# Adding the causal mask of a prompt's scores with weights of 64 rows instead of 128

## The chip, the cores and the metric

The kernel runs on one core of a Trainium2 chip. The metric is the device time of one launch in microseconds; before the change the median of three runs is 2850.2 us (2848.51 to 2850.68). The profile shows one execution, whose span from the first to the last instruction is 2845.2 us, at a mean granted TensorE clock of 0.998.

## The reference, cut to what matters

One inference step of a decoder with two layers: a short gated convolution with a feed forward behind it, then differential attention with a feed forward behind it. There are 1024 new prompt tokens and 8 sequences of 8 sample tokens, each with 2048 cached keys and values in pages of 128. The change lies in the attention of the prompt:

```python
s = jnp.einsum('bqhd,bkhd->bhqk', q, k).astype(jnp.float32) * SCALE      # head dim 64, 2 * 8 heads
s = jnp.where(mask[None, None], s, jnp.finfo(jnp.float32).min)           # causal
p = jax.nn.softmax(s, axis=-1)
a = p[:, :, 0] - lam * p[:, :, 1]                                        # the two halves of a head
return jnp.einsum('bhqk,bkhe->bqhe', a, v.astype(jnp.float32))
```

A head has two halves (here c = 0 and c = 1), each with scores and a softmax of its own; their difference weighs the values.

## The kernel before, in words

Nearly all of the time is matmul in float32 with a high and a low part for each operand (three products). The stages follow each other: the convolution and the first feed forward, the projections of the prompt (line L687), the attention of the prompt with the attention of the samples mixed in, the output projection (L140) and the second feed forward.

The attention of the prompt goes over 8 heads and, in each, over 8 blocks of 128 queries (i = 4, 5, 6, 7, 0, 1, 2, 3), so 64 blocks. For a block, `scores` makes for each half a 128 x n matrix in PSUM, n = 128 (i + 1). A half has 64 dimensions, so the contraction has 64 rows: half 0 has its operands in partitions 0 to 63 and half 1 in 64 to 127, and the two matmuls of a pair stand next to each other (L752). Up to n = 512 both halves share one PSUM tile of two banks; above that each half has a tile of two banks, and there are two such tiles in all. The mask is then added by TensorE itself: an identity `idb` of 128 x 128 in bfloat16 as weights, and the mask of the diagonal block `cmask` as the moving operand, accumulated onto the last 128 columns, once for each half (L755). Then VectorE takes the maximum of each row (L757 or L759), ScalarE the exponential (L763), and the result waits. One or two blocks later `mixed` turns it with TensorE (L780) and `values` multiplies with the values (L787); `place` (L806) puts four finished blocks back; `head_turn` (L726) turns the next head's queries and keys.

Between these stand steps of the samples: `step(x)` adds x to a credit, and for each full 1 one step of a generator is recorded, which weighs one page of values (L590, four column tiles of 32) and multiplies one page of keys (L532, eight matmuls in the same tiles). Before the change `step(0.72)` stands behind each of the two masks, so 1.44 steps per block. Pages come through six buffers of 512 KB, and SyncE issues their loads (L511) in a fixed order, each as soon as its buffer is free.

In this stage the order on TensorE, VectorE, ScalarE and GpSimd is set by a scheduler from the order in the program and the dependences; SyncE's queue is kept as written. In the profile a matmul's shape has the part of the array that it uses ahead: `64*128` is 64 rows (a half's scores), `128*128` the whole array, `128*32` a column tile of the samples.

Of the kernel before, what the change touches and what calls it, by code (L numbers as in the profile page):

```python
# [11 lines left out]
BF16 = mybir.dt.bfloat16  # L12
# [6 lines left out]
P = 128  # L19
# [30 lines left out]
def decoder_kernel(ctx: ExitStack, tc: tile.TileContext, i_: dict, o_: dict):  # L50
    nc = tc.nc
    PE, ACT, DVE, POOL, SP = nc.tensor, nc.scalar, nc.vector, nc.gpsimd, nc.sync
# [25 lines left out]
    def load_split(src, width=D, eng=None, sub=None, lo_raw=False):  # L78
        raw = rawp.tile([P, width], F32, name="raw", tag="raw")
        (eng or SP).dma_start(raw, src)  # L80
        hi = wsp.tile([P, width], F32R, name="whi", tag="w")
        lp, tag = (rawp, "raw") if lo_raw else (wsp, "w")
        lo = lp.tile([P, width], F32R, name="wlo", tag=tag)
        split_to(hi, lo, raw, sub)
        return hi, lo, raw

    def passes(ah, al, bh, bl):
        return ((ah, bh), (ah, bl), (al, bh))
# [151 lines left out]

    xsT = cst.tile([P, KT, NS], F32, name="xsT")

    # ------------------------------------------------------------ layer 0
    with tc.tile_pool(name="accp", bufs=1) as accp, \
         ExitStack() as conv_stack, \
         tc.tile_pool(name="pout0", bufs=4, space=PSUM) as pout, \
# [2 lines left out]
        tp = conv_stack.enter_context(tc.tile_pool(name="tp", bufs=1, reuse_waits="tile"))  # L249
        st = stream(accp, "acc")  # L250

        # ---- short convolution
        taps = accp.tile([P, KT, 3], F32, name="taps")
        stT = accp.tile([P, KT, NSEQ, 2], F32, name="stT")
        cpT = accp.tile([P, KT, 2], F32, name="cpT")
# [99 lines left out]
        POOL.dma_start(o_["conv_p"], cpT)  # L355
        POOL.dma_start(o_["conv_s"], csT)

        # ---- feed forward
        def ffn(layer, pin, pout, hp, tp, st, ln):
            def feature(f):  # L360
                sg = tp.tile([P, NT], F32, name="sg", tag="gb", bufs=1)
                hh = hp.tile([P, NT], F32R, name="hh", tag="h")
                hl = hp.tile([P, NT], F32R, name="hl", tag="h")
                hs = hp.tile([P, NS], F32, name="hs", tag="hs", bufs=5)

                def put_g(c0, cw, ps):
                    ACT.activation(sg[:, c0:c0 + cw], ps, AF.Silu)  # L367

                def put_u(c0, cw, ps):
                    cs = slice(c0, c0 + cw)  # L370
                    hf = tp.tile([P, 364], F32, name="hf", tag="hf")
                    DVE.tensor_tensor(hf[:, :cw], ps, sg[:, cs], op=ALU.mult)  # L372
                    split_to(hh[:, cs], hl[:, cs], hf[:, :cw])
                    if c0 == 0:
                        POOL.tensor_copy(hs, hf[:, 0:NS])

                in_type(pin, i_["wfi"][layer, 2 * f], put_g)
                in_type(pin, i_["wfi"][layer, 2 * f + 1], put_u)
                return hh, hl, hs

            run_chunks(pout, st, (2,) * 9 + (4,), feature, i_["wfo"][layer], ln)
# [4 lines left out]
            ffn(0, pin, pout, hp, tp, st,  # L386
                norm(1, tp, accp, "f32", x2_dram, lambda x: SP.dma_start(s2_dram, x)))

    # ------------------------------------------------------------ layer 1 attention
    with tc.tile_pool(name="kvp", bufs=1, reuse_waits="tile") as kvp, \  # L390
         tc.tile_pool(name="ap", bufs=1, reuse_waits="tile") as ap, \
         tc.tile_pool(name="ap2", bufs=2, reuse_waits="tile") as ap2, \
# [8 lines left out]
            return kvp.tile(shape, dtype, name=name, tag=f"kv{next(kv_slot)}")  # L401

        w0 = [load_split(i_["wqkv"][0, kh].rearrange("p k c -> p (k c)"), eng=POOL, lo_raw=kh == 0) for kh in range(2)]
        # constants of this phase
        idb = ap2.tile([P, P], BF16, name="idb", bufs=1)
        cmask = ap2.tile([P, P], BF16, name="cmask", bufs=1)
        smask = ap.tile([P, 120], F32, name="smask")
        sel = ap.tile([P, 4], F32, name="sel")
        cmb = ap.tile([P, NS], F32, name="cmb")
# [10 lines left out]
        ccA = ap.tile([P, 2], F32, name="ccA")  # L420

        def constants():
            for tl, nm in ((idb, "idb"), (cmask, "cmask"), (smask, "smask"), (sel, "sel"), (cmb, "cmb"),
                           (ropp, "ropp"), (rops, "rops"), (ptab, "ptab")):
                SP.dma_start(tl, i_[nm])
            SP.dma_start(gs, i_["subg"])
            SP.dma_start(lamt, i_["lam"].partition_broadcast(P))
            DVE.tensor_scalar(gs, gs, 1.0 - LAM_INIT, None, op0=ALU.mult)
            DVE.tensor_tensor(lpr, lamt[:, 0:4:2, :], lamt[:, 1:4:2, :], op=ALU.mult)
            DVE.tensor_reduce(lsum, lpr, axis=AX.X, op=ALU.add)  # L430
            ACT.activation(lex, lsum, AF.Exp)
            DVE.tensor_tensor(nlam, lex[:, 1:2], lex[:, 0:1], op=ALU.subtract)
            DVE.tensor_scalar(nlam, nlam, LAM_INIT, None, op0=ALU.subtract)
            DVE.scalar_tensor_tensor(ccA, sel[:, 2:4], nlam[:, 0:1], sel[:, 0:2], op0=ALU.mult, op1=ALU.add)
# [9 lines left out]
            DVE.tensor_tensor(vb[..., 8:16], dst[..., 0:8], sin[..., 8:16], op=ALU.mult)  # L444
            DVE.tensor_tensor(x12, va, vb, op=ALU.add)

        # ---- sample tokens: projections folded over two partition halves, then paged attention
        vs = ap.tile([P, 512], F32, name="vs")
        qT = ap.tile([P, 4, P], F32, name="qT")
        kTs = ap.tile([P, 4, P], F32, name="kTs")  # L450
# [208 lines left out]
        def step(x):  # L659
            credit[0] += x  # L660
            while credit[0] >= 1.0:
                credit[0] -= 1.0
                next(samp, None)

        RATE3 = 0.76
        # ---- prompt projections
        with tc.manual_schedule(engines={mybir.EngineType.PE}):
            for pr in range(4):
                for ty, dst in enumerate((q_dram, o_["k_p"], o_["v_p"])):
# [6 lines left out]
                    for tg in range(2):  # L676
# [3 lines left out]
                        for kh, t in [(kh, t) for kh in range(2) for t in range(4)] if first else [(None, t) for t in range(4)]:  # L680
# [3 lines left out]
                            for k in range(KT) if kh is None else range(4 * kh, 4 * kh + 4):  # L684
                                cs = slice((k % 4) * 256, (k % 4) * 256 + 256)
                                for n, (a, b_) in enumerate(passes(xTh, xTl, his[k // 4], los[k // 4])):
                                    PE.matmul(ps[t][:, t % 2, :256], a[:, k, t0:t0 + P], b_[:, cs],  # L687
                                              start=(k == 0 and n == 0), stop=(k == KT - 1 and n == 2),
                                              skip_group_check=True)
# [14 lines left out]
                        cols = slice(pr * 256, pr * 256 + 256)  # L704
                        POOL.dma_start(dst[rows, cols].rearrange("(t p) c -> p t c", p=P), nat)

        # ---- prompt attention
        def head_load(h):
            cols = slice(h * P, h * P + P)
            out = []  # L710
            for src, nm in ((q_dram, "qn"), (o_["k_p"], "kn"), (o_["v_p"], "vn")):
                t = (rawp if nm != "vn" else ap2).tile([P, KT, P], F32, name=nm, tag="raw" if nm != "vn" else "vn")
                POOL.dma_start(t, src[:, cols].rearrange("(t p) c -> p t c", p=P))
                out.append(t)
            return out
# [16 lines left out]
        def scores(q, k, i):  # L732
            n = (i + 1) * P
            nb = 1 if n <= 512 else 2
            w = n // nb
            kf = [x.rearrange("p t c -> p (t c)") for x in k]
            nms = sml.tile([P, 2], F32, name="pnm", tag="pnm")
            l = sml.tile([P, 2], F32, name="pl", tag="pl")
            Ps = []
            ps = pt = None  # L740
            svs = []
            for c in range(2):
                if nb == 2 or c == 0:
                    ps = ps2.tile([P, 2, 512], F32, name="psS2", tag="s2")
                    pt = ap2.tile([P, NP], F32, name="pexp", tag="pr", bufs=4)
                svs.append(ps[:, :, :w] if nb == 2 else ps[:, c:c + 1, :w])
                Ps.append((svs[c], pt[:, :n] if nb == 2 else pt[:, c * 512:c * 512 + n]))
            for bk in range(nb):
                for m, (a, b_) in enumerate(passes(q[0], q[1], kf[0], kf[1])):
                    for c in range(2):  # L750
                        cp = slice(c * 64, c * 64 + 64)
                        PE.matmul(svs[c][:, bk, :], a[cp, i, :], b_[cp, bk * w:bk * w + w],  # L752
                                  start=(m == 0), stop=(m == 2), skip_group_check=True)
            for c in range(2):
                PE.matmul(svs[c][:, nb - 1, w - P:w], idb, cmask, start=False, stop=True, skip_group_check=True)  # L755
                if nb == 2:
                    DVE.tensor_reduce(nms[:, c:c + 1], svs[c], axis=AX.XY, op=ALU.max, negate=True)  # L757
                elif c == 1:
                    DVE.tensor_reduce(nms, ps[:, :, :w], axis=AX.X, op=ALU.max, negate=True)  # L759
                step(RATE4)  # L760
            for c in range(2):
                sv, pv = Ps[c]
                ACT.activation(pv.rearrange("p (b w) -> p b w", b=nb), sv, AF.Exp,  # L763
                               bias=nms[:, c:c + 1], accum_out=l[:, c:c + 1])
            ls, Ps = l, [p_ for _, p_ in Ps]
            rl = sml.tile([P, 2], F32, name="prl", tag="prl")
            DVE.reciprocal(rl, ls)
            r1 = rl[:, 0:1]
            rr = sml.tile([P, 1], F32, name="prr", tag="prr")
            DVE.scalar_tensor_tensor(rr, ls[:, 0:1], rl[:, 1:2], nlam, op0=ALU.mult, op1=ALU.mult)  # L770
            DVE.scalar_tensor_tensor(Ps[0], Ps[1], rr[:, 0:1], Ps[0], op0=ALU.mult, op1=ALU.add)
            return r1, Ps[0]
# [39 lines left out]
        RATE4 = 0.72  # L812
# [27 lines left out]
                place(*done)  # L840
        step(200)

    # ------------------------------------------------------------ attention output, feed forward
    with tc.tile_pool(name="accq", bufs=1, reuse_waits="tile") as accp, \
         tc.tile_pool(name="hq", bufs=8, reuse_waits="tile") as hp, \
         tc.tile_pool(name="tq", bufs=2, reuse_waits="tile") as tp, \
# [109 lines left out]
```

## Time and profile before

| what | value |
|---|---|
| median of the runs | 2850.2 us |
| span of the profiled execution | 2845.2 us |
| median of the runs less that span | 5.0 us |
| TensorE busy in that span | 2810.5 us, 99% |
| VectorE, ScalarE, GpSimd busy | 1190.4, 704.7, 253.7 us |
| first matmul of the prompt's scores to the last mask | 1574.4 to 1937.3 us |
| mask matmuls (L755) | 128, each 219 to 232 ns from start to end |

The profile gives no time of its own for the whole launch of the profiled execution, only its span; what lies around the span is taken as the 5.0 us by which the median is above it. A matmul's duration there reaches from its first operand to its last result, and the next one starts before it ends; so what a matmul costs is read from one start to the next, in the timeline, and not from its duration.

### The profile page before, as it was taken

To read this page: it belongs to the slowest core of one execution; us is meant where nothing else is said; L and a number is where in the kernel's file an instruction comes from. 1 tells how busy PE (TensorE), PEld (TensorE's weight loads), DVE (VectorE), ACT (ScalarE), POOL (GpSimd) and SP (SyncE) were. 2 spreads that over 40 slices of the span, in tenths; PEclk is the share of its full clock that TensorE was granted. 3 is DMA by queue.
4 is the path that set the end of the run, shared out by engine and by line. 5 is a ranking of instruction groups with operands and counts; after the bars stand their busy time and mean duration, and the time that the engine had idled before them with its cause. 6 is when DMAs were issued, how large, how long until landed. Compare 5 with 4: busy or idle time off the path is not lost.

```text
span 2845.2 us, 45546 instructions
## 1 busy us (share of the span) xinstructions
PE 2810.5 (99%) x19092; PEld 2474.1 (87%) x19092; DVE 1190.4 (42%) x2083; ACT 704.7 (25%) x1366; POOL 253.7 (9%) x517
## 2 busy tenths in 40 slices
PE   9999999999999999999999999999999999999998
PEld 9998989999999999879888666667799999999996
DVE  4435373333333332722222566676733333333325
ACT  3111141111111111312221455562311111111111
POOL 0000020000000000311111223231200000000002
PEclk9999999999999999999999999999999999999999
DMA  6111021111111111486777888761211111111102
GB/s 225 39 39 57 25 83 42 44 43 44 45 43 45 45 44 31 137 284 205 268 273 259 290 275 297 275 211 60 75 52 45 45 45 45 45 45 45 45 30 78
DMA packets 87456, 307.50 MB, mean 108 GB/s; under 512 B 10929, under 2 KB 11586, under 8 KB 87250
## 3 DMA queue, kind: packets, MB, share of 16 engines
q1 hardware_dynamic: 76194, 265.45, 27.7%
q0 software_dynamic: 10624, 38.35, 4.1%
q8 instruction: 150, 2.46, 0.4%
q10 hardware_dynamic: 432, 0.79, 0.1%
q14 instruction: 56, 0.46, 0.0%
HBM read 282.46 MB, written 22.09 MB: 107 GB/s over the span
## 4 chain that ended last, share of the span: by engine, by line
PE 93%; DMA 2%; DVE 1%; POOL 1%; ACT 1%; issue 1%; SPq 0%; POOLq 0%; DVEq 0%; ACTq 0%
PE pin L104 46%; PE pout L140 21%; PE psqkv L687 9%; PE psS L752 3%; PE psO L590 3%; PE pso L787 2%; PE psS L532 2%; PE pouts L125 2%; PE psaT L780 1%; PE psq L474 1%; DMA vpg<-cv 1%; PE psS L755 1%; POOL rs_t L93 1%; PE pstr L726 0%; PE ptr L216 0%
## 5 line engine op out<-in xcount | busy, mean ns | idle before, releaser
L104 PE MATMUL pin<-xTh,whi 128*128 128x362 f32 (+1 forms) x2688 | 876.0, 326 | 6.4 <-ACT xTh L75 6.4
L104 PE MATMUL pin<-xTl,whi 128*128 128x362 f32 (+1 forms) x2688 | 875.6, 326 | 0.3 <-DVE xTl L76 0.3
L104 PE MATMUL pin<-xTh,wlo 128*128 128x362 f32 (+1 forms) x2688 | 875.0, 326 | 0.0
L76 DVE TENSOR_TENSOR wlo<-raw,whi 128x1024 fp32r<-128x1024 f32 (+1 forms) x197 | 239.9, 1218 | 687.9 <-PE pin L104 400.7
L104 PEld LDWEIGHTS pin<-xTh,whi 128*128 128x128 f32 x2688 | 505.6, 188 | 7.4 <-ACT xTh L75 6.4
L104 PEld LDWEIGHTS pin<-xTl,whi 128*128 128x128 f32 x2688 | 505.6, 188 | 1.6 <-DVE xTl L76 0.7
L104 PEld LDWEIGHTS pin<-xTh,wlo 128*128 128x128 f32 x2688 | 505.6, 188 | 0.1
L75 ACT CAST whi<-raw 128x1024 fp32r<-128x1024 f32 (+1 forms) x197 | 203.8, 1045 | 729.7 <-PE pout L140 379.0
L140 PE MATMUL pout<-whi,hh 128*128 128x512 f32 x704 | 279.3, 397 | 0.0
L140 PE MATMUL pout<-whi,hl 128*128 128x512 f32 x704 | 278.6, 396 | 0.0
L140 PE MATMUL pout<-wlo,hh 128*128 128x512 f32 x704 | 278.0, 395 | 0.0
L687 PE MATMUL psqkv<-whi,xTh 128*128 128x256 f32 x768 | 222.5, 290 | 0.0
L687 PE MATMUL psqkv<-wlo,xTh 128*128 128x256 f32 x768 | 214.5, 279 | 0.0
L687 PE MATMUL psqkv<-whi,xTl 128*128 128x256 f32 x768 | 214.4, 279 | 0.0
L140 PEld LDWEIGHTS pout<-whi,hh 128*128 128x128 f32 x704 | 132.6, 188 | 45.7 <-issue 14.6
L140 PEld LDWEIGHTS pout<-whi,hl 128*128 128x128 f32 x704 | 132.7, 189 | 31.2 <-issue 1.6
L367 ACT ACTIVATE sg<-pin 128x364 f32<-128x364 f32 x132 | 62.6, 474 | 388.6 <-PE pin L104 388.6
L140 PEld LDWEIGHTS pout<-wlo,hh 128*128 128x128 f32 x704 | 132.6, 188 | 30.1
L687 PEld LDWEIGHTS psqkv<-whi,xTh 128*128 128x128 f32 x768 | 144.5, 188 | 15.6 <-issue 14.5
L372 DVE TENSOR_TENSOR hf<-pin,sg 128x364 f32<-128x364 f32 x132 | 70.4, 533 | 207.0 <-PE pin L104 207.0
L115 DVE TENSOR_TENSOR acc<-acc,pout 128x512 f32<-128x512 f32 x160 | 109.3, 687 | 93.5 <-PE pout L140 93.5
L687 PEld LDWEIGHTS psqkv<-wlo,xTh 128*128 128x128 f32 x768 | 144.7, 188 | 0.0
(216 smaller groups left out, 3236.7 us busy)
## 6 DMA issues: line engine op xcount, KB each, us to landing
kpg<-ck SPq DMA_DIRECT2D x128, 512.0 KB, 5.6
vpg<-cv SPq DMA_DIRECT2D x128, 512.0 KB, 5.0
raw<-wfi SPq DMA_DIRECT2D x88, 512.0 KB, 4.0
raw<-wfo SPq DMA_DIRECT2D x44, 512.0 KB, 3.7
raw<-wqkv POOLq DMA_DIRECT2D x24, 512.0 KB, 5.6
raws<-wqkv SPq DMA_DIRECT2D x24, 512.0 KB, 6.4
raw<-wci SPq DMA_DIRECT2D x23, 512.0 KB, 3.7
acc<-xn SPq DMA_DIRECT2D x8, 512.0 KB, 9.7
```

Of the source, the lines that this page charges most:

```text
L75: ACT.copy(hi, src)
L76: (eng or DVE).tensor_tensor(lo, src, fv(hi), op=ALU.subtract)
L104: PE.matmul(ps[:, :cw], a[:, k * P:(k + 1) * P], b[:, k, c0:c0 + cw], start=(k == 0 and n == 0), stop=(k == KT - 1 and n == 2),)
L115: DVE.tensor_tensor(a, a, ps, op=ALU.add)
L125: PE.matmul(ps[half * NS:half * NS + NS, :], hs, raw[:, half * 512:half * 512 + 512], start=(j == 0), stop=(j == last), skip_group_check=True)
L140: PE.matmul(ps, a[:, t0:t0 + P], b[:, cs], start=(j == 0 and n == 0), stop=(j == last and n == 2))
L367: ACT.activation(sg[:, c0:c0 + cw], ps, AF.Silu)
L372: DVE.tensor_tensor(hf[:, :cw], ps, sg[:, cs], op=ALU.mult)
L532: PE.matmul(ps[32 * t:32 * t + 32, n, :], qp[:, 2 * t + h2, :], kp[:, 2 * t + h2, :], start=(h2 == 0), stop=(h2 == 1), skip_group_check=True)
L590: PE.matmul(O[32 * t:32 * t + 32, :], PT[:, p, 32 * t:32 * t + 32], vp[:, 2 * t:2 * t + 2, :].rearrange("p h d -> p (h d)"), start=(p == 0 ...
L687: PE.matmul(ps[t][:, t % 2, :256], a[:, k, t0:t0 + P], b_[:, cs], start=(k == 0 and n == 0), stop=(k == KT - 1 and n == 2), skip_group_che ...
L752: PE.matmul(svs[c][:, bk, :], a[cp, i, :], b_[cp, bk * w:bk * w + w], start=(m == 0), stop=(m == 2), skip_group_check=True)
```

## The change

`idb` and `cmask` are held twice, in partitions 0 to 63 and in 64 to 127, with their rows 0 to 63 and 64 to 127 side by side; each needs two loads of 64 partitions instead of one. The mask of a half is added by two matmuls with 64 rows of weights each: the first adds rows 0 to 63 of the mask over all 128 columns, the second rows 64 to 127 over the last 64 columns alone, where these rows have something to mask. Half 0 uses partitions 0 to 63 and half 1 partitions 64 to 127, as in the scores. All four stand together, and the steps of the samples, `step(2 * RATE4)`, come behind them. Comment lines were taken out too.

```diff
-        idb = ap2.tile([P, P], BF16, name="idb", bufs=1)
-        cmask = ap2.tile([P, P], BF16, name="cmask", bufs=1)
+        idb = ap2.tile([P, 2, P], BF16, name="idb", bufs=1)
+        cmask = ap2.tile([P, 2, P], BF16, name="cmask", bufs=1)
...
-            for tl, nm in ((idb, "idb"), (cmask, "cmask"), (smask, "smask"), (sel, "sel"), (cmb, "cmb"),
+            for tl, nm in ((idb, "idb"), (cmask, "cmask")):
+                for c in range(2):
+                    SP.dma_start(tl[c * 64:c * 64 + 64], i_[nm].rearrange("(r p) k -> p r k", r=2))
+            for tl, nm in ((smask, "smask"), (sel, "sel"), (cmb, "cmb"),
                            (ropp, "ropp"), (rops, "rops"), (ptab, "ptab")):
                 SP.dma_start(tl, i_[nm])
...
+            for r in range(2):
+                for c in range(2):
+                    cp = slice(c * 64, c * 64 + 64)
+                    PE.matmul(svs[c][:, nb - 1, w - P + 64 * r:w], idb[cp, r, :], cmask[cp, r, 64 * r:],
+                              start=False, stop=(r == 1), skip_group_check=True)
             for c in range(2):
-                PE.matmul(svs[c][:, nb - 1, w - P:w], idb, cmask, start=False, stop=True, skip_group_check=True)
                 if nb == 2:
                     DVE.tensor_reduce(nms[:, c:c + 1], svs[c], axis=AX.XY, op=ALU.max, negate=True)
                 elif c == 1:
                     DVE.tensor_reduce(nms, ps[:, :, :w], axis=AX.X, op=ALU.max, negate=True)
-                step(RATE4)
+            step(2 * RATE4)
```

Where the order on TensorE changes is seen at three places. The lines of the changed kernel are 4 higher from the samples on (L752 is L756 there, L590 L594, L532 L536) and 9 higher behind the masks (L780 is L789, L787 L796); the new masks are L762.

First, TensorE, the third head's block of i = 2. Before:

```order
L752 MATMUL psS_16828<-qtl,qth 128x384 x2
L752 MATMUL psS_16828<-qth,qtl 128x384 x2
L755 LDWEIGHTS idb
L755 MATMUL psS_16828<-cmask,idb 128x128
L590 MATMUL psO<-vpg,PT 32x256 x4
L532 MATMUL psS<-kpg,qpad_9080 32x128 x8
L755 LDWEIGHTS idb
L755 MATMUL psS_16828<-cmask,idb 128x128
L787 MATMUL pso<-vn,aT 128x128
L726 MATMUL pstr<-ident,kn 128x128 x4
```

and in the changed kernel:

```order
L756 MATMUL psS_16874<-qtl,qth 128x384 x2
L756 MATMUL psS_16874<-qth,qtl 128x384 x2
L762 LDWEIGHTS idb
L762 MATMUL psS_16874<-cmask,idb 128x128
L762 LDWEIGHTS idb
L762 MATMUL psS_16874<-cmask,idb 128x128
L762 LDWEIGHTS idb
L762 MATMUL psS_16874<-cmask,idb 128x64
L762 LDWEIGHTS idb
L762 MATMUL psS_16874<-cmask,idb 128x64
L594 MATMUL psO<-vpg,PT 32x256 x4
L536 MATMUL psS<-kpg,qpad_9080 32x128 x8
```

The step of the samples stood between the two masks and now stands behind all four; `pso` (L796 there) follows it.

Second, TensorE, the next block (i = 3), which has two steps of the samples. Before:

```order
L755 LDWEIGHTS idb
L755 MATMUL psS_16922<-cmask,idb 128x128
L590 MATMUL psO<-vpg,PT 32x256 x4
L532 MATMUL psS<-kpg,qpad_9080 32x128 x8
L755 LDWEIGHTS idb
L755 MATMUL psS_16922<-cmask,idb 128x128
L590 MATMUL psO<-vpg,PT 32x256 x4
L532 MATMUL psS<-kpg,qpad_9080 32x128 x8
L787 MATMUL pso<-vn,aT 128x128 x2
```

and in the changed kernel, from the second half of the masks on:

```order
L762 LDWEIGHTS idb
L762 MATMUL psS_16970<-cmask,idb 128x64
L762 LDWEIGHTS idb
L762 MATMUL psS_16970<-cmask,idb 128x64
L594 MATMUL psO<-vpg,PT 32x256 x4
L536 MATMUL psS<-kpg,qpad_9080 32x128 x8
L594 MATMUL psO<-vpg,PT 32x256 x4
L536 MATMUL psS<-kpg,qpad_9080 32x128 x8
L796 MATMUL pso<-vn,aT 128x128 x2
```

The two steps now follow each other with no mask between them.

Third, SyncE, the constants of the attention, before the samples' first loads:

```order
L426 DMA idb<-idb 64x2x128 x2
L426 DMA cmask<-cmask 64x2x128 x2
L171 DMA x_dram<-acc_101 128x1024
L429 DMA smask<-smask 128x120
L429 DMA sel<-sel 128x4
```

Before, the first two rows were one load each, of 128 x 128, at the same place.

## The prediction

> **What bounds the kernel now.** First the page's totals, its chain of work and its rate of transfers by slices; then one stretch of the view by windows, from the first score to the last mask.
>
> ```profile
> span 2845.2 us, 45546 instructions
> PE 2810.5 (99%) x19092; PEld 2474.1 (87%) x19092; DVE 1190.4 (42%) x2083; ACT 704.7 (25%) x1366; POOL 253.7 (9%) x517
> ...
> GB/s 225 39 39 57 25 83 42 44 43 44 45 43 45 45 44 31 137 284 205 268 273 259 290 275 297 275 211 60 75 52 45 45 45 45 45 45 45 45 30 78
> ...
> PE 93%; DMA 2%; DVE 1%; POOL 1%; ACT 1%; issue 1%; SPq 0%; POOLq 0%; DVEq 0%; ACTq 0%
> ```
>
> ```profile
> 1574.00:1938.00 364.00, 358.94 (x3690) 245.97 (x3690) 247.94 (x497) 209.34 (x582) 103.65 (x229) 1.00 0.77 263
> ```
>
> TensorE is busy for 99% of the span and is 93% of the chain that ended last. In the stage of the change, 364 us long, its columns are TensorE 358.94 busy, its weight loads 245.97, VectorE 247.94, ScalarE 209.34, GpSimd 103.65, then the clock (1.00), the share of the DMA engines (0.77) and GB/s (263). No other engine is near full. What TensorE waited for there, by the view of waits:
>
> ```profile
> PE psO L590 <- DMA vpg<-cv: 2.0, 3, 1.3
> PE psS L532 <- DMA kpg<-ck: 1.3, 2, 0.8
> PE pstr L726 <- DVE ost L790: 0.5, 2, 0.2
> PE psaT L780 <- ACT aT L781: 0.4, 1, 0.4
> PE psS L752 <- ACT pexp L763: 0.3, 1, 0.3
> PE psS L752 <- ACT qth L728: 0.2, 1, 0.2
> ```
>
> That is all: 4.7 us of 364. So this stage's length is the sum of the steps from one matmul's start to the next, and what the change takes out of these steps it takes out of the time. But "busy" says little about the steps. The view of waits for the weight loads shows where they are long:
>
> ```profile
> PEld L755 <- issue: 19.5, 75, 0.4
> ```
>
> 75 of the 128 mask matmuls' weight loads start after 0.26 us on average in which they wait for no other engine. The timeline shows what this is (start, duration, instruction, count; the duration is a latency, only starts are compared):
>
> ```profile
> 1700.90 0.28 PE L752 MATMUL psS<-qtl,qth 64*128 64x256 f32 x2
> 1701.02 0.29 PE L752 MATMUL psS<-qth,qtl 64*128 64x256 f32 x2
> 1701.24 0.29 PE L755 MATMUL psS<-cmask,idb 128*128 128x128 bf16 x2
> 1701.45 0.64 PE L590 MATMUL psO<-vpg,PT 128*32 128x256 f32 x8
> ...
> 1706.25 0.33 PE L780 MATMUL psaT<-ident,pexp 128*128 128x128 f32 x1
> 1706.51 0.44 PE L752 MATMUL psS<-qth 64*128 64x384 f32 x2
> 1706.79 0.33 PE L752 MATMUL psS<-qtl,qth 64*128 64x384 f32 x2
> 1706.96 0.34 PE L752 MATMUL psS<-qth,qtl 64*128 64x384 f32 x2
> 1707.23 0.23 PE L755 MATMUL psS<-cmask,idb 128*128 128x128 bf16 x1
> 1707.39 0.64 PE L590 MATMUL psO<-vpg,PT 128*32 128x256 f32 x8
> 1707.84 0.62 PE L532 MATMUL psS<-kpg,qpad 128*32 128x128 f32 x16
> 1708.39 0.23 PE L755 MATMUL psS<-cmask,idb 128*128 128x128 bf16 x1
> 1708.46 0.44 PE L787 MATMUL pso<-vn,aT 128*128 128x128 f32 x2
> ```
>
> A pair of scores of 384 columns takes 0.17 when the next pair has the same shape of array (1706.79 to 1706.96), and 0.27 when a mask over all 128 rows follows (to 1707.23). With 256 columns it is 0.12 against 0.22 (1700.90, 1701.02, 1701.24). The mask in front of a column tile takes 0.16 (1707.23 to 1707.39); in front of a matmul over the whole array 0.07 (1708.39 to 1708.46), though the type changes there too. So **a switch between `64*128`, `128*128` and `128*32` costs about 0.10 us**, and the first score pair behind a switch (1706.51, after a turn over the whole array) takes 0.28 instead of 0.17, another 0.11.
>
> **The change part by part.**
>
> *Switches.* I count, in the two orders on TensorE from the first score to the last mask, the neighbours of different shape: 486 before, 367 after. Of the 486, 94 lead into a mask (64 of them straight from the scores), 73 out of one and 319 stand elsewhere; of the 367 it is 2, 63 and 302. The masks now have the scores' shape, so the switch from scores to mask is gone in all but two places, and a step between two masks no longer makes two switches of its own. 119 switches by 0.10 us are -11.9 us. Only mask, scores and column tiles are read above; that the others cost as much is an assumption for the 17 that vanish elsewhere. Behind a switch, 11 fewer score pairs start (11 by 0.11, -1.2), 10 more `pso` do and 24 fewer groups of pages; none of these last two is priced by a row above, and I put the whole at -1, with -2 and +1 as ends.
>
> *The masks themselves.* Before: two masks and the switch behind them take 0.21 (1701.24 to 1701.45), so one takes about 0.06: 128 by 0.06 is 7.7 us. After, a block has a pair over 128 columns and a pair over 64. No row shows bfloat16 weights in 64 rows. If a pair runs together as the scores' pairs do, the 128 columns take 0.06 (half of the 0.12 for 256) and the 64 columns between 0.03 and 0.06: 0.10 a block, 64 by 0.10 is 6.4 us, so -1.3. The lower end is 0.09 a block (-1.9). For the upper end I take that each of the two pairs needs the 0.12 of the 256-column pair, because loading, not streaming, sets the pace: 0.24 a block, 15.4 us, so +7.7. I stay near the lower end, since the row that is nearest in type, the mask with 128 rows, has its next mask ready within 0.06.
>
> ```profile
> L755 PEld LDWEIGHTS <-idb x128: 94/96/100, 1576.4 to 1937.2; 128*128 128x128 bf16 x128
> ...
> L752 PEld LDWEIGHTS psS<-qth x192: 182/183/188, 1574.4 to 1935.6; 64*128 64x128 f32 x192
> ```
>
> The first row is a mask's weight load, 0.096 us from start to end with 128 rows; 128 such loads become 256. [...]
>
> *The steps of the samples.* Their number stays (64 by 1.44, 92 calls) and so does the block that each stands in; 28 blocks have two. They move behind the second mask, so the maximum over both halves at up to 512 columns can start a step earlier, and the reduction of half 0 above that no later than about 0.1 us. What covers the chain reduction, exponential, next scores in the same tile is the same work as before (steps, turns, values); it is not shortened by the switch in front of the mask, which lies ahead of the chain. It is 0.3 us of waiting now (the fifth row of waits); I add 0.5.
>
> *Pages.* SyncE's order of pages is unchanged. In 14 us less the same bytes need 263 by 364/350, 274 GB/s; the slices of the page reach 297. The waits for pages are 3.3 us now, and a page is asked for well ahead:
>
> ```profile
> vpg<-cv SPq DMA_DIRECT2D x83, 512.0 KB, 5.2
> kpg<-ck SPq DMA_DIRECT2D x65, 512.0 KB, 6.0
> ```
>
> ```profile
> SPq L511 <- PE psO L590: 134.7, 55, 7.5
> ```
>
> A page lands 5.2 to 6.0 us after its issue, and SyncE's queue stands 134.7 us of 364 waiting for a buffer to be freed, not for transfers. Six buffers are three steps' worth, which at 364/92, about 4.0 us a step, is about 12 us from a buffer's freeing to the use of its next page, twice the landing. So nothing is added here.
>
> *Constants.* Two more loads on SyncE:
>
> ```profile
> 1191.45 0.78 SPq L425 DMA_DIRECT2D cmask<-cmask  x1
> 1199.02 0.33 SPq L171 DMA_DIRECT2D x_dram<-acc  x1
> ```
>
> After `cmask` that queue waits until 1199.02 for a row of VectorE. Two issues of at most 0.78 fit into the 6.8 us between, and their first use is at 1576: nothing. Without that cover they would put off the samples' weights by 1.6 us.
>
> *Sum.* -11.9 - 1 - 1.3 + 0.5 is -13.7, rounded to -14: a span of 2831.2. Around the span lie the 5.0 us by which the median of the runs is above it, so the time is **2836 us**. Its own range is 2830 (every term at its better end, and some switches dearer than 0.10) to 2840.
>
> **The rivals.** *One: the gain is halved.* It was not the shape but the change from float32 to bfloat16 in front of the mask that cost the 0.10, and 62 of those steps remain: +6.2; or the pairs of masks are held up at 0.12 each: +7.7 and +1.3. The time is 2842 to 2845. For it: float32 to bfloat16 within one shape stands in no row. Against it: bfloat16 to float32 does (0.07, no gap).
>
> *Two: slower, by the pages.* In 28 blocks two steps stand together without a mask between, and the second waits for its pages. The longest wait for a page now is 1.3 us; at 0.75 in each of the 28 it is 21 us, and the time 2857. It decides from 0.5 us a pair of steps (14/28). For it: the waits for pages are most of what TensorE waits for, at a DMA share of 0.77. Against it: such a pair was apart by one mask only before (0.07 to 0.16 us in the rows above), and the queue has slack.
>
> *Three: no change, by the weight loads.* Each of the 128 added loads shows in full, 0.096 us: +12.3, a time of 2848. For it: 64 rows load no faster (0.183 us in the second row on loads). Against it: the scores' pairs, two loads each, follow each other at 0.12, less than one load's duration, so loads do overlap. [...]
>
> *Four: the switches only turn into waits*, because VectorE and ScalarE set the stage's pace through the two tiles of scores: 2846 to 2850. Against it: they are busy 68% and 58% of the stage (247.94 and 209.34 of 364).
>
> **How the numbers follow.** Forecast 0.62, one 0.19, two 0.07, three and four 0.06 each. The measurement can tell 0.2%, 5.7 us, from no change, so faster means under 2844.5. The forecast and nearly all of rival one are faster: 0.80. Three, four and the rest of one are within: 0.13. Two is slower: 0.07. The range is the forecast's own, stretched to the end of rival one: 2830 to 2846, with some 0.8 of the chance.
>
> **What would show it.** The changed profile should have 128 more matmuls on TensorE; 364 us from first score to last mask should become about 350; the wait "issue" in front of the masks' weight loads, 19.5 us, should nearly vanish; the last score pair in front of a mask should take 0.17 with 384 columns, and the four masks with the switch behind them about 0.20. If the step in front of the mask is still 0.27, or the masks follow each other at 0.12, rival one or three holds; if TensorE's waits for pages rise from 3.3 us to 20, rival two. The forecast is wrong if the stage shrinks and the end does not, which would put a wait behind the stage.

## The result and the profile after

The changed kernel takes 2832.0 us (median of four runs, 2831.6 to 2836.8) against 2849.8 us beside it: a ratio of 0.9945, with a 95% interval of 0.9931 to 0.9959. By the ratio it is some 16 us faster; the forecast was 2836 with a range of 2830 to 2846.

The page of the changed kernel, its span and its totals:

```profile
span 2835.1 us, 45793 instructions
PE 2798.8 (99%) x19220; PEld 2473.4 (87%) x19220; DVE 1188.2 (42%) x2083; ACT 703.3 (25%) x1366; POOL 253.6 (9%) x517
```

There are 128 more matmuls and 128 more weight loads (19220 against 19092), and TensorE is busy for 11.7 us less. This execution took 2836.8 us, so 1.7 us lie around its span; in the other three it is 1.7 us too. It is also the slowest of the four, which the last section comes back to. The stage from the first score to the last mask, by the view by windows:

```profile
1575.40:1926.20 350.80, 344.87 (x3815) 244.94 (x3816) 245.18 (x496) 206.67 (x578) 102.37 (x228) 0.99 0.79 272
```

Its columns are the stretch and its length, the busy times of TensorE, its weight loads, VectorE, ScalarE and GpSimd, then TensorE's granted clock, the share of the DMA engines and GB/s. The stage takes 350.8 us, 12.1 less than the 362.9 of before, at 272 GB/s where 274 was worked out. What TensorE still waited for in it, the first three rows of the view of waits:

```profile
PE psO L594 <- DMA vpg<-cv: 1.7, 1, 1.7
PE psS L756 <- ACT qth L732: 0.8, 3, 0.5
PE psS L756 <- ACT pexp L772: 0.8, 2, 0.5
```

and the row of the same view for the masks' weight loads:

```profile
PEld L762 <- issue: 6.6, 30, 0.4
```

The wait of 19.5 us in 75 places is 6.6 us in 30; the waits for pages have not grown (1.7 us, before 3.3). The timeline shows the third head's block of i = 2 and, behind it, the pages of the block of i = 3:

```profile
1701.06 0.44 PE L756 MATMUL psS<-qth 64*128 64x384 f32 x2
1701.34 0.34 PE L756 MATMUL psS<-qtl,qth 64*128 64x384 f32 x2
1701.52 0.33 PE L756 MATMUL psS<-qth,qtl 64*128 64x384 f32 x2
1701.69 0.26 PE L762 MATMUL psS<-cmask,idb 64*128 64x128 bf16 x4
1701.88 0.64 PE L594 MATMUL psO<-vpg,PT 128*32 128x256 f32 x8
...
1705.65 0.62 PE L536 MATMUL psS<-kpg,qpad 128*32 128x128 f32 x16
1706.09 0.61 PE L594 MATMUL psO<-vpg,PT 128*32 128x256 f32 x8
1706.52 0.62 PE L536 MATMUL psS<-kpg,qpad 128*32 128x128 f32 x16
1707.07 0.71 PE L796 MATMUL pso<-vn,aT 128*128 128x128 f32 x4
```

The last pair of scores in front of the masks takes 0.17 (1701.52 to 1701.69), as between two pairs of scores, where it took 0.27. The four masks and the switch behind them take 0.19. So the step into the masks costs nothing any more, though it still goes from float32 to bfloat16: it was the shape. The lower rows price a switch elsewhere: sixteen key matmuls take 0.44 when pages follow (1705.65 to 1706.09) and 0.55 when `pso` does (1706.52 to 1707.07), so a switch there costs 0.11.

### The profile page after: what moved, and what is told of

It reads as the page before. It is cut to its first block, busy times and chain, and to the rows that moved or that the text cites. A ratio compares the mean times of both kernels' runs of the same rounds, so it can differ in the third digit from the quotient of the medians.

```text
span 2835.1 us, 45793 instructions
## 1 busy us (share of the span) xinstructions
PE 2798.8 (99%) x19220; PEld 2473.4 (87%) x19220; DVE 1188.2 (42%) x2083; ACT 703.3 (25%) x1366; POOL 253.6 (9%) x517
## 4 chain that ended last, share of the span: by engine, by line
PE 91%; DVE 2%; ACT 2%; DMA 2%; POOL 1%; issue 1%; SPq 0%; POOLq 0%; DVEq 0%; ACTq 0%
PE pin L104 46%; PE pout L140 21%; PE psqkv L691 10%; PE psS L756 2%; PE psO L594 2%; PE pso L796 2%; PE psS L536 2%; PE pouts L125 2%; PE psaT L789 1%; PE psq L478 1%; POOL rs_t L93 1%; PE psT L583 0%; PE ptr L216 0%; ACT pexp L772 0%; ACT junk L159 0%
## 5 line engine op out<-in xcount | busy, mean ns | idle before, releaser
L140 PE MATMUL pout<-whi,hh 128*128 128x512 f32 x704 | 278.7, 396 | 0.1
L140 PE MATMUL pout<-whi,hl 128*128 128x512 f32 x704 | 278.3, 395 | 0.0
L140 PE MATMUL pout<-wlo,hh 128*128 128x512 f32 x704 | 277.6, 394 | 0.0
L140 PEld LDWEIGHTS pout<-whi,hh 128*128 128x128 f32 x704 | 132.4, 188 | 46.3 <-issue 14.6
L140 PEld LDWEIGHTS pout<-whi,hl 128*128 128x128 f32 x704 | 132.4, 188 | 30.9 <-issue 1.6
L140 PEld LDWEIGHTS pout<-wlo,hh 128*128 128x128 f32 x704 | 132.4, 188 | 30.3
```

Of the source, the lines that this page charges most:

```text
L140: PE.matmul(ps, a[:, t0:t0 + P], b[:, cs], start=(j == 0 and n == 0), stop=(j == last and n == 2))
```

## The experiments

Each was timed beside the kernel before on the same chip; a ratio is to that kernel. All diffs are against the changed kernel. Where steps are added up below, they are the steps from one matmul's start to the next over the stage, each counted to the first of the two.

### The change repeated

No edit.

> The changed kernel once more, to have its distance from the kernel before with a closer interval and beside the other runs of this batch. Theory (the gain is the switches of the array's shape that are gone, 119 by 0.10 us, and dearer starts behind them): 15 to 18 us less than before, about 0.994 of it. If the first profile's 10 us between the two spans were the true gain, it would be 0.9965.

Measured: 2830.0 us against 2847.0, ratio 0.9944 (0.9930 to 0.9957); the stage 350.2 us. As expected. The gain of 16 us is larger than the 12 to 13 us by which this stage and the first one are shorter than the 362.9 us of before; that is taken up in the last experiment.

### The order alone: masks of 128 rows, together, the steps behind both

```diff
-            for r in range(2):
-                for c in range(2):
-                    cp = slice(c * 64, c * 64 + 64)
-                    PE.matmul(svs[c][:, nb - 1, w - P + 64 * r:w], idb[cp, r, :], cmask[cp, r, 64 * r:],
-                              start=False, stop=(r == 1), skip_group_check=True)
+            for c in range(2):
+                PE.matmul(svs[c][:, nb - 1, w - P:w], idb, cmask, start=False, stop=True, skip_group_check=True)
```

and the constants held and loaded as before.

> The kernel before with its masks over 128 rows, but both masks of a block together and the steps of the samples behind both. That is the change's order without its 64 rows. Switches of shape in the order from the first score to the last mask: 417 (before 486, changed 367). Theory of the switches: 69 fewer by 0.10 to 0.12 us, so 7 to 9 us less than before, about half of the change's gain. Rival (the gain comes from the steps' new place, by way of earlier maxima and fewer waits): the whole 15 to 18 us. Rival (the gain comes from the masks' smaller size): no gain.

Measured: 2834.3 us, ratio 0.9956 (0.9943 to 0.9970), 12.6 us less; the stage by the view by windows, and the same block as above in the timeline:

```profile
1573.40:1925.10 351.70, 348.11 (x3680) 242.97 (x3680) 245.26 (x494) 207.78 (x580) 106.91 (x228) 1.00 0.78 271
```

```profile
1699.84 0.34 PE L752 MATMUL psS<-qth,qtl 64*128 64x384 f32 x2
1700.12 0.28 PE L755 MATMUL psS<-cmask,idb 128*128 128x128 bf16 x2
1700.33 0.64 PE L590 MATMUL psO<-vpg,PT 128*32 128x256 f32 x8
```

The switch in front of the masks is there (0.28 from the last scores), and two masks with the switch behind them take 0.21. Yet most of the gain is there too, 4 to 6 us more than expected: 12.6 lies between the 7 to 9 us of the switches and the 15 to 18 of the rival, by which the steps' new place brings it all. Its time and the changed kernel's, 2830.0 us on the same chip, are 4 us apart, but the intervals of the two ratios overlap (0.9943 to 0.9970 and 0.9930 to 0.9957). This kernel runs 415 switches in the stage where before ran 484. 69 by 0.10 explain 6.9 of the 12 us by which its stage is shorter than the 363.7 us that the kernel before took on the same footing (last experiment); TensorE's own waits are 2.4 us less (3.6 against 6.0), and some 3 us I can't place. This stage has one stretch of 3.4 us at half clock in it (last section); whatever that cost comes on top.

### The weights alone: masks of 64 rows, the steps between the halves

```diff
-            for r in range(2):
-                for c in range(2):
-                    cp = slice(c * 64, c * 64 + 64)
+            for c in range(2):
+                cp = slice(c * 64, c * 64 + 64)
+                for r in range(2):
...
-            for c in range(2):
                 if nb == 2:
...
-            step(2 * RATE4)
+                step(RATE4)
```

> The changed kernel with its masks of 64 rows, but the masks of half 0, a call of the samples' steps, the masks of half 1 and another call, as before the change. That is the change's 64 rows without its order. Switches: 435 (before 486). Theory of the switches: 51 fewer by 0.10 to 0.12 us, and some 2 us from the masks themselves where they stand together, so 5 to 8 us less than before. Rival (the steps' new place alone): no gain. Rival (the masks' size alone): the whole 15 to 18 us.

Measured: 2840.4 us, ratio 0.9977 (0.9967 to 0.9988), 6.6 us less, as expected. Its stage, and the block of i = 2:

```profile
1573.40:1929.30 355.90, 351.00 (x3814) 244.60 (x3813) 246.45 (x495) 207.78 (x580) 102.62 (x228) 1.00 0.78 268
```

```profile
1702.47 0.34 PE L756 MATMUL psS<-qth,qtl 64*128 64x384 f32 x2
1702.65 0.26 PE L762 MATMUL psS<-cmask,idb 64*128 64x128 bf16 x2
1702.83 0.64 PE L594 MATMUL psO<-vpg,PT 128*32 128x256 f32 x8
1703.29 0.62 PE L536 MATMUL psS<-kpg,qpad 128*32 128x128 f32 x16
1703.84 0.26 PE L762 MATMUL psS<-cmask,idb 64*128 64x128 bf16 x2
1704.02 0.49 PE L795 MATMUL pso<-vn,aT 128*128 128x128 f32 x2
```

The step into the first mask has gone (0.18), but the two masks of a half, which use the same rows of the array, follow each other alone: 0.18 with the switch, twice, where four masks together take 0.19. What the weights save in front of the masks is in part lost again behind them.

### Fewest switches: TensorE's order as written

```diff
+        with tc.manual_schedule(engines={mybir.EngineType.PE}):
             for h in range(NH):
```

The loop over heads and blocks stands inside it, otherwise unchanged; the scheduler no longer moves TensorE's instructions there.

> The changed kernel with TensorE's order in the attention of the prompt as written in the program and not the scheduler's: scores, masks, steps, values, turns, one group after the other. Switches: 229 (changed 367). If switches were all, 138 fewer by 0.10 us and their dearer starts would give about 22 us less than the changed kernel, 2810. Against that stand waits: the next scores of half 1 come after some 2.1 to 3.0 us of other work and need two reductions and an exponential, 2.9 to 3.6 us, so I expect some 0.8 us of waiting in three blocks of each head, 20 us in all, and a time within 6 us of the changed kernel. The waits in the profile, by ScalarE's exponentials, tell the two apart.

Measured: 2844.2 us, ratio 0.9993 (0.9983 to 1.0003): with 227 switches instead of 362 it is no faster than the kernel before, and 14 us slower than the changed kernel on the same chip (2830.0), where I had expected at most 6. Its stage and TensorE's longest waits in it:

```profile
1570.30:1934.30 364.00, 322.84 (x3840) 237.82 (x3840) 246.64 (x497) 208.08 (x582) 102.25 (x230) 0.97 0.76 262
```

```profile
PE psaT L789 <- DVE xTl L819: 7.8, 6, 1.3
PE psS L536 <- ACT S L540: 7.0, 5, 2.4
PE psO L594 <- DVE PT L584: 4.3, 4, 1.7
PE psaT L789 <- DVE ost L799: 4.3, 8, 1.5
PE psS L756 <- ACT pexp L772: 3.7, 6, 0.9
```

TensorE is busy for 322.8 us only, 22 less than in the changed kernel, and waits for 41.2 us, mostly for copies and reductions on VectorE and ScalarE; the exponentials are 3.7 us of it, so the expected reason was not the main one. The stage also holds six stretches of 3.4 us at half clock (its mean clock is 0.97), each worth up to 1.7 us. I read this so: the switches are real costs, and many of them are the price at which the scheduler fills waits.

### Which half leads

In 38 of the 64 blocks of the changed kernel the masks run as two pairs, in 0.20 us with the switch. In the others the halves are out of step, as in this block of i = 5 of the changed kernel:

```profile
1629.20 0.34 PE L756 MATMUL psS<-qtl,qth 64*128 64x384 f32 x1
1629.27 0.26 PE L762 MATMUL psS<-cmask,idb 64*128 64x128 bf16 x2
1629.38 0.34 PE L756 MATMUL psS<-qth,qtl 64*128 64x384 f32 x1
1629.56 0.26 PE L762 MATMUL psS<-cmask,idb 64*128 64x128 bf16 x2
1629.75 0.42 PE L594 MATMUL psO<-vpg,PT 128*32 128x256 f32 x3
```

The matmuls of a pair no longer start together (1629.20 and 1629.38), and one half is through with its scores first: its two masks begin at 1629.27, the other half's last scores come behind them, and its masks at 1629.56. In 11 blocks the four masks follow each other singly, in 0.37 us on average. The experiment starts the pairs with half 1 in the blocks above 512 columns:

```diff
-                    for c in range(2):
+                    lead = None
+                    for c in (1, 0) if nb == 2 else (0, 1):
                         cp = slice(c * 64, c * 64 + 64)
-                        PE.matmul(svs[c][:, bk, :], a[cp, i, :], b_[cp, bk * w:bk * w + w],
-                                  start=(m == 0), stop=(m == 2), skip_group_check=True)
+                        with tc.issue_after(lead.ins) if lead is not None and nb == 2 else ExitStack():
+                            lead = PE.matmul(svs[c][:, bk, :], a[cp, i, :], b_[cp, bk * w:bk * w + w],
+                                             start=(m == 0), stop=(m == 2), skip_group_check=True)
```

> The changed kernel, but where a block has two tiles of scores (more than 512 columns) each matmul of half 1 is issued before its partner of half 0; nothing else in the order moves (367 switches as in the changed kernel). In the changed kernel's trace the four masks with the switch behind them take 0.20 us where the halves run as pairs (38 of 64 blocks) and 0.37 where they run one after the other. Theory: half 0 gets its tile first and runs ahead of half 1, and the masks at the end pay for it; with half 1, whose tile comes free last, in front, the halves start together, nearly all blocks have paired masks, and the stage is 26 by 0.17, some 4 us, shorter, less up to 1 us of waiting for the later tile: 2 to 4 us less than the changed kernel. Rival: the masks are split for another reason (the weights, or the order of the masks); then pairs stay at about 38 and the time does not move.

Measured: 2832.8 us, ratio 0.9950 (0.9937 to 0.9962), no difference that the times can tell. Its stage of 352.6 us, at a mean clock of 0.99, has 10 us at half clock in it and can't be compared. 34 blocks run in pairs instead of 38, where the theory expected nearly all 64: which half is issued first does not decide whether they run in step, and what does is open.

### The second mask over all 128 columns

```diff
-                    PE.matmul(svs[c][:, nb - 1, w - P + 64 * r:w], idb[cp, r, :], cmask[cp, r, 64 * r:],
+                    PE.matmul(svs[c][:, nb - 1, w - P:w], idb[cp, r, :], cmask[cp, r, :],
```

> The changed kernel, but the second mask of a half goes over all 128 columns instead of the last 64, with zeros in the first 64. Theory (the masks' time is streaming, 0.03 us for 64 columns, once for a pair): 64 by 0.03 is about 2 us more than the changed kernel, a little more where the halves do not run as pairs. Rival (loading the weights sets the pace of the masks): no difference.

Measured: 2832.0 us, ratio 0.9952 (0.9940 to 0.9965), no difference that the times can tell. In the block of i = 2:

```profile
1698.39 0.28 PE L762 MATMUL psS<-cmask,idb 64*128 64x128 bf16 x4
1698.61 0.64 PE L594 MATMUL psO<-vpg,PT 128*32 128x256 f32 x8
```

Four masks and the switch take 0.22 against 0.19, and all masks of the stage 18.9 us against 16.7 to 17.1, the 2 us that were expected. So half the columns save 0.03 a block, and the second pair's pace is set by its columns, not by its weight loads.

### Steps of the samples in larger lumps

```diff
-            step(2 * RATE4)
+            if i % 2:
+                step(4 * RATE4)
```

> The changed kernel, but the samples' steps are recorded behind every second block, 2.88 on average, not 1.44 behind each. The scheduler spreads them again: 386 switches instead of 367. Theory of the switches: 19 by 0.10 and dearer starts, 2 to 3 us more than the changed kernel; pages still come in time (six buffers are three steps), TensorE's waits for them stay under 6 us. Rival (steps in a row starve the pages): waits for pages of 10 us and more, and as much more time.

```diff
-            step(2 * RATE4)
+            if i % 4 == 3:
+                step(8 * RATE4)
```

> The same with the steps behind every fourth block, 5.76 on average, which is nearly twice what the six buffers hold. 405 switches. Theory: 4 to 6 us by the switches, and now waits for pages as well, about a landing (5 us) less the time of three steps (3 us) in each of 16 rows of steps where the scheduler keeps them together, up to 30 us: 10 to 35 us more than the changed kernel. If even this shows no waits for pages, the rival of the pages is out in every form.

Measured: 2843.1 us, ratio 0.9986 (0.9978 to 0.9995), with steps behind every second block, and 2861.4 us, 1.0058 (1.0045 to 1.0071), behind every fourth. The stage of the first, and the longest of TensorE's waits in it, the one for pages of values:

```profile
1571.90:1933.20 361.30, 350.75 (x3813) 248.68 (x3812) 244.26 (x494) 206.44 (x577) 99.32 (x227) 0.99 0.75 262
```

```profile
PE psO L594 <- DMA vpg<-cv: 3.0, 3, 1.8
```

and of the second:

```profile
1572.80:1943.90 371.10, 353.71 (x3808) 250.68 (x3809) 245.28 (x493) 207.55 (x574) 101.67 (x224) 1.00 0.71 252
```

```profile
PE psO L594 <- DMA vpg<-cv: 6.0, 8, 1.3
PE psS L756 <- ACT pexp L773: 4.0, 8, 1.2
```

Grouping steps has a price, but the pages are the smaller part of it: 3.0 us of waits for the values and 1.0 for the keys with two blocks' steps in a lump, 6.0 and 1.5 us with four, where the stage is 10.5 and 20.3 us longer than the changed kernel's 350.8 us. TensorE's waits in all are 10.6 and 17.4 us against 5.9, and its busy time goes up by 6 and 9 us with 384 and 403 switches against 362, of which 22 and 41 switches by 0.13 us are 3 and 5. That lumps leave less to fill the waits for VectorE and ScalarE with, and break up what is left, is how I read it; no run shows it by itself. For the first I had expected 2 to 3 us and missed it. For the second I had expected 10 to 35, and by the ratios it is some 30 us, but not by the pages as I had thought; of what the stage does not show, 3.6 us are one wait behind it, for an output of the samples from GpSimd.

### Both kernels side by side

The times differ by more than the two first profiles' stages, so both kernels were profiled twice more on one chip, without an edit.

> The kernel before, unchanged, to have its stages on the same chip as the changed kernel's. The times differ by 16 to 17 us between the two kernels, the one pair of profiles by 12 to 13 in the stage from the first score to the last mask, so 3 to 4 us are not placed. Theory (the stage alone): the stage is 363 us within 1, as in the first profile, the time outside it differs from the changed kernel's by under 1.5 us at the same granted clock, and the missing 3 to 4 us were the difference of two chips and of the clock. Rival one: the stage of the kernel before is longer here, 365 to 367. Rival two: the stages around it are longer than the changed kernel's by 3 us at the same clock, most of it between the last mask and the end.

> The changed kernel on the same chip. Theory: the stage takes 350 to 351 us, 12 to 13 less than that of the kernel before beside it, and the time outside it is the same within 1.5 us once the stretches at half clock are taken off. Rival one: 15 to 16 less in the stage. Rival two: 12 to 13 less in the stage, 3 less outside it.

> A second execution of the kernel before, to see how far the stage and the time outside it vary between executions of one kernel: by the theory the stage by under 1 us, apart from 1.7 us for each stretch of 3.4 us at half clock, and the time outside it by 2 to 4 us.

> A second execution of the changed kernel; by the theory the stage is 350 to 351 us again, by under 1 us, and the time outside it varies by 2 to 4 us.

Measured: the kernel before 2847.2 and 2846.5 us (ratios 1.0001 and 0.9999 to its own other runs), the changed one 2832.8 us, 0.9957 (0.9944 to 0.9971), and 2830.7 us, 0.9952 (0.9929 to 0.9974). The stage by windows, in the first profile of the kernel before:

```profile
1573.60:1937.30 363.70, 357.71 (x3683) 244.95 (x3683) 246.67 (x495) 208.78 (x580) 102.30 (x228) 1.00 0.77 262
```

its second,

```profile
1573.30:1936.50 363.20, 358.74 (x3683) 246.02 (x3683) 246.75 (x495) 208.79 (x580) 102.70 (x228) 1.00 0.77 263
```

the first of the changed kernel,

```profile
1573.10:1921.10 348.00, 341.61 (x3817) 242.62 (x3816) 244.84 (x496) 206.58 (x578) 103.13 (x228) 1.00 0.80 274
```

and its second:

```profile
1575.30:1923.30 348.00, 341.64 (x3815) 242.56 (x3816) 244.82 (x496) 206.78 (x578) 103.28 (x228) 1.00 0.79 274
```

The stage lost 15.2 to 15.7 us, not 12 to 13: the size of rival one, though not in its form, since the kernel before takes what it took. The changed kernel's stage is 348.0, not 350.8; its first profile held two stretches at half clock (last section), which these two don't have. The second profile of the kernel before does have one, from 1584.1 to 1587.4 us, so up to 1.7 of its 363.2 us are that; the two profiles of it without one, 362.9 and 363.7, give 14.9 to 15.7. Outside the stage the spans leave 2479.3 and 2479.5 us before and 2477.3 and 2480.4 after (2843.0, 2842.7, 2825.3 and 2828.4 less the stage): no difference beyond the 3 us by which the changed kernel's own two differ. So the whole gain lies in the stage, as far as these profiles can tell.

Its steps, added up by what they belong to, in us (the kernel with masks of 128 rows together has one stretch at half clock in it, worth up to 1.7):

| | before | 64 rows alone | together alone | changed |
|---|---|---|---|---|
| scores | 91.6 | 78.8 | 90.7 | 78.1 |
| masks | 16.2 | 20.3 | 12.9 | 16.8 |
| pages, values and keys | 96.8 | 96.8 | 90.3 | 91.8 |
| all else | 159.1 | 160.0 | 157.8 | 161.3 |
| stage | 363.7 | 355.9 | 351.7 | 348.0 |
| switches run | 484 | 427 | 415 | 362 |

Weights of 64 rows take 13 us out of the scores' steps, whatever the order. Keeping masks together takes 5 to 6.5 us out of the pages' steps and 3.3 to 3.5 us out of the masks', whatever the weights. The two gains don't add up in time (7.8 and 12.0 make 19.8, both together 15.7): with the masks together, 8.9 of the 12.6 us that the weights take out of the scores' steps come back, as 3.9 in the masks, 1.5 in the pages and 3.5 in all else.

Part of that last row is work of the next stage, which the scheduler lets in ahead of the last mask: 7 matmuls of the output projection (L140) before, 9 with the weights alone, 4 with the order alone and 12 in the changed kernel, whose steps are 2.0, 2.6, 1.1 and 3.2 us. Without them the order alone takes 11.1 us out of the stage, the weights alone 8.4 and both 16.9. So the order alone brings two thirds of the gain or more, and the weights, on top of it, 5.8 us, or 1.7 less if the stretch at half clock cost all that it can.

## Why the prediction was right

The time is 4 us from the forecast, and the sign, the place and the mechanism, switches of shape that go, are as predicted. How the gain divides between the weights and the order is not as the single price per switch would have it, and that the sum came so near is in part luck. By its steps:

**The bound.** That the stage is the sum of the steps from start to start held: it lost 14.9 to 15.7 us, and the time 12 to 16 us by the ratios of the four comparisons.

**Switches.** 119 were counted to go in the orders; 122 went in the trace (484 to 362). The price of 0.10 read from masks, scores and column tiles was confirmed where it had been assumed, at 0.11 between pages and `pso`. The scores' and masks' steps together lost 12.9 us, where the terms on them (64 switches straight from the scores 6.4, 10 out of masks 1.0, 11 dear starts 1.2, the masks' own 1.3) give 9.9; all else lost 2.8 us, where the terms give 3.8. Over all, 15.7 us by 122 switches are 0.13 each, so 0.10 was a little low. But this is an average of unequal parts: the order alone has 69 switches fewer and takes 11.1 us, 0.16 each, and the weights on top of it 53 fewer and 5.8 us, 0.11 each at most. The sum had no term for what the order gains beyond its switches, 2.4 us of it fewer waits, and the masks' term below was off the other way; I can't place the rest instruction by instruction.

**The masks themselves** were the term with the wrong sign: forecast -1.3, measured about +1.8 (from 16.2 less 73 switches out of masks by 0.10 to 16.8 less 61). The working holds for the 38 blocks in which masks run in pairs, 0.19 with the switch, at the lower end that was chosen. What it assumed without a row is that all blocks do; in the rest they run singly or between the other half's last scores.

**The steps of the samples, the pages, the constants.** The allowance of 0.5 for waits is of the right size: TensorE waits for 6.4 us in the stage against 6.0 in one pair of profiles and 4.5 in the other. Pages cost nothing at 274 GB/s, and the first score starts at 1573 to 1575 us as before. That steps moved together could cost was the right concern, but by the wrong cause: in larger lumps most of the loss is not the pages.

**Around the span** the prediction put 5.0 us, from one profile against the median of other runs; it is 1.7 to 2.1 us in every execution whose span is listed. The profiled execution of before was thus some 3 us faster than the median one. This does not explain the 4 us by which the forecast was late, for 2836 is the median of before less 14 whichever way the 5.0 is read. Between the medians of this comparison the kernel lost 17.8 us (2849.8 to 2832.0) against 13.7 in the sum; the stage accounts for 1 to 2 us of the difference, and the rest is within the spread of single executions (2841 to 2852 us in 23 of the kernel before). The span, forecast at 2831.2, was 2829.9 to 2835.1 in the four executions; that it fits is luck in part, since the forecast started from a fast execution and its sum was too small.

**The rivals.** One: its first half is refuted by the step from float32 to bfloat16 at 0.17, the same as between scores; its second half, pairs held at 0.12 each, by 0.19 for all four and the switch, and by the 0.03 that half the columns save, in the blocks that run in pairs; in the 11 where masks run singly, at 0.37, something of its size is there. Two: the waits for pages stayed at 1.7 to 2.5 us, not 21. Three: 128 more loads take no time that shows, since TensorE's weight loads in the stage are busy for 242.6 us, 2.3 less than before, and the stage is 15 shorter. That 64 rows load no faster is so: a mask's load takes 0.095 us there against 0.096 with 128 rows. The 0.183 that the prediction gives for it is of float32, where a load with 128 rows takes 0.188 (L687, before). Four: the waits on VectorE and ScalarE did not take the gain here; with TensorE's order as written, waits of 41.2 us and the stretches at half clock take all of it.

## What to carry to other kernels

Where an engine is busy for 99% of the time, look at the steps from start to start: a change of the array's shape cost 0.10 to 0.11 us in the rows here, a few hundred times, and showed only as "issue" in front of weight loads. Give a short matmul the shape of its neighbours, and keep small matmuls of one shape together, which alone brought two thirds of the gain here or more; but count the switches in the order that runs, and don't force the fewest: with 227 switches instead of 362 this kernel was 14 us slower. A difference of a few us between two single profiles is no measure of a gain: profile each kernel more than once on one chip, and look at the clock's column first.

## What the hardware did that I had not expected

TensorE's clock falls to half (0.50 to 0.51) for single short stretches in the middle of dense work, of 3.4 us each and in the stage once of 6.8 (with half 1 first, where the stage's mean clock is 0.99); behind the stage the first profile of the changed kernel has another of 6.8 (1938.6 to 1945.4 us, at 0.50). That first profile, by windows:

```profile
1586.90:1590.30 3.40, 3.40 (x32) 2.54 (x30) 0.78 (x1) 1.07 (x4) 0.00 (x0) 0.51 1.04 408
1853.20:1856.60 3.40, 3.40 (x22) 2.26 (x19) 1.86 (x5) 2.15 (x5) 0.00 (x0) 0.50 0.28 46
```

Stretches near the same places in the first of the two profiles with a stage of 348.0:

```profile
1583.50:1586.90 3.40, 3.40 (x44) 2.41 (x36) 1.36 (x2) 2.79 (x8) 1.12 (x3) 1.00 1.03 410
1853.20:1856.60 3.40, 3.40 (x38) 2.02 (x38) 3.40 (x5) 1.98 (x5) 0.00 (x0) 1.00 0.08 27
```

The seventh column of numbers is the clock. At half clock TensorE works on 32 and 22 matmuls in 3.4 us, where the later profile has 44 and 38 (of not quite the same work); half of 3.4 us, 1.7 us, is by that clock the most that a stretch can cost. Each follows waits of TensorE, in brackets in the timeline of the first profile:

```profile
1585.30 0.64 PE L594 MATMUL psO<-vpg,PT 128*32 128x256 f32 x8 [1.71 <-DMA vpg<-cv]
...
1850.68 0.41 PE L756 MATMUL psS<-qth 64*128 64x320 f32 x1 [0.55 <-ACT pexp L772]
...
1851.55 0.41 PE L756 MATMUL psS<-qth 64*128 64x320 f32 x2 [0.16 <-ACT qth L732]
```

Up to 1.7 us of waiting stand in the 3.4 us ahead of the first stretch, 0.7 ahead of the second, 2.0 ahead of the one behind the stage. But a wait of 1.3 us passed without one in the profile with 348.0, and of the two extra profiles of the kernel before the first passed a wait of 1.7 us at full clock, while the second's of 1.8 us was followed by half clock; so the length of the wait alone does not decide it. How many an execution catches differs: none, one or two in the changed kernel's stage, six in the kernel with the order as written (its mean clock there is 0.97), and runs of the kernel before spread from 2841 to 2852 us at mean clocks of 0.999 to 0.995.

The price of a change of shape is 0.10 to 0.11 us in the rows, 0.13 over the whole gain. Pairs in step take four masks and a switch in 0.19 us, but the two halves can fall out of step, as in the block of i = 5 above (starts at 1629.20 and 1629.38), and they stay so there to its end.
